# Row order of the loads of rotated queries and keys: 32 rows outermost, four parts within

## Chip, core and metric

One core of a Trainium2 chip runs one transformer layer. The metric is the time of one execution in microseconds of device time (us), the median of several. Before the change it is 2902.48 us, the median of three runs between 2901.76 and 2904.4.

## What is computed

A sequence of 1024 positions with 1024 features goes through a feed-forward block, a mixing block and a second feed-forward block. The mixing block holds two attentions: a differential one with 8 heads (phase "da" below) and one with 16 heads whose output is a gated sum of a compressed, a selected and a window branch (phase "ns"). The change touches only how queries and keys reach the score products. In the reference these are the lines

```python
s = jnp.einsum('bqhcd,bkhcd->bhcqk', qb, k).astype(jnp.float32) * scale      # da
s = jnp.einsum('bqgjd,bqgnld->bqgjnl', qb, kg).astype(jnp.float32) * scale   # ns, selected
s = jnp.einsum('bqgjd,bkgd->bqgjk', qb, kb).astype(jnp.float32) * scale      # ns, window
```

Each is a sum over the 64 features d of a head, after the rotation of queries and keys. The order of the terms in that sum is free.

## The kernel before

**Operands in two parts.** Products are taken to about single precision by cutting each operand into a rounded part and a remainder (`split`, L85 and L89: ScalarE, ACT in the profile, makes the rounded part, VectorE, DVE, the remainder). A weight product is three TensorE (PE) matmuls (L52 to L54).

**Rotated queries and keys pass through memory.** `rope_pair` computes two blocks of 128 columns of the input projection, rotates them, splits them and stores them (L635) to scratch tensors in device memory: `s_q` and `s_k` (one of each for every pair of da heads), `s_qns` for the ns queries, `s_kv` for the ns keys. Their shape is `[h, a, s, d, t]`:

- `h`: rounded part or remainder (queries have the rounded part once more at the end, so that `h = 0, 1` is rounded and remainder, and `h = 1, 2` remainder and rounded);
- `a`: first or second half of the 64 features, `s`: one of four vectors, `d`: 32 features, `t`: 1024 positions.

For a fixed `s`, the step from one `d` to the next is a row of 1024 numbers, 4 KB; the step from one `(h, a)` to the next is 4 x 32 x 1024 numbers, 512 KiB.

**Loads for the scores.** A score product contracts over 128 partitions: two `h` times two `a` times 32 `d`. The loads put them there in the order `(h a) d`, so that partition 32 j + d holds row d of part j. There are four places:

- `da_queries` (L928): four loads of 128 rows of 256 positions for each head and quarter of the sequence, a pool of 4 buffers (`B_DQ`), two loads to a buffer;
- `da_load_parts` (L1031): two key loads of 128 rows of 1024 positions for each head, a pool of 4 buffers (`B_DK`); the values `vt` follow at L1038;
- `ns_load_key` (L1047): four key loads of the same size, made during da head 4;
- `ns_queries` (L1072): two loads of 128 rows of 512 positions for each head and half.

`scores` multiplies (L909): the two passes of a score tile `S` use the queries with `h = 0, 1` and with `h = 1, 2` against the same key tile. Queries and keys of one product always come through the loads above, so their partitions are ordered alike. DVE then adds the mask and takes the row minimum (L916), ACT the exponential (L918); POOL and DVE scale, PE transposes (L964), ACT and DVE split again, and PE multiplies by the values (L991 to L993 in da, L1146 and L1147 in ns).

**Fillers.** Between score tiles the PE runs pieces of projections (`Filler`): units of `rope_pair` and `v_da_unit` for later heads, then gates. Their weights `wst` are loaded at L1200 and split by ACT at L1210 and DVE at L85. The value units end in transposes (L653), a split into `vh` and `vl`, and stores (L658); the gates in stores at L745. The finished da heads go out at L1018.

**What sets the order.** Every engine runs its instructions in the order of the program text as a scheduler laid it out at build time, and waits on semaphores. All transfers, loads and stores, are issued by SyncE (SP) alone, one after another; an issue that does not get through holds all later ones. A transfer is carried out by the core's 16 DMA engines.

Of the kernel before, what the change touches and what calls it, by code (L numbers as in the profile page):

```python
# [7 lines left out]
F32 = mybir.dt.float32  # L8
# [912 lines left out]
def da_queries(K, h, m):  # L921
    nc = K.nc
    qt = []
    p, s0 = h // 2, (h % 2) * 2
    for c in range(2):
        t = K.qp.tile([P, 2, 2 * P], F32R, tag="q", name="qt")
        for z in range(2):
            nc.sync.dma_start(out=t[:, z].bitcast(F32),  # L928
                              in_=K.s_q[p][z:z + 2, :, s0 + c, :, m * 256:(m + 1) * 256].rearrange("h a d t -> (h a) d t"))
        qt.append(t)  # L930
    return qt

# [88 lines left out]
def da_load(K, h):  # L1021
    drain([da_load_parts(K, h)])


def da_load_parts(K, h):
    nc = K.nc
    p, s0 = h // 2, (h % 2) * 2
    K.k = []
    for c in range(2):
        t = K.kp.tile([P, T], F32R, tag="k", name="kt")  # L1030
        nc.sync.dma_start(out=t.bitcast(F32), in_=K.s_k[p][:, :, s0 + c].rearrange("h a d t -> (h a) d t"))  # L1031
        K.k.append(t)
        yield
    K.v = []
    K.vv[h] = K.v
    for hl in range(2):
        t = K.vp.tile([P, 8, P], F32R, tag="v", name="vt")
        nc.sync.dma_start(out=t.bitcast(F32), in_=K.s_v[h][hl])  # L1038
        K.v.append(t)
        yield  # L1040


def ns_load_key(K, i):
    g, br = i // 2, i % 2
    pool, tag = [(K.rope, "cR"), (K.rope, "sR"), (K.mp, "m13"), (K.mp, "rh")][i]
    t = pool.tile([P, T], F32R, tag=tag, name="kt")
    order_after(K, K.nc.sync.dma_start(out=t.bitcast(F32), in_=K.s_kv[:, :, br * 2 + g].rearrange("h a d t -> (h a) d t")),  # L1047
                K.last)
    K.nk[g, br] = t

# [17 lines left out]
def ns_queries(K, hd, H):  # L1068
    qt = []
    for z in range(2):  # L1070
        t = K.qp[hd % 2].tile([P, TB], F32R, tag=f"q{z}", name="qt")
        K.nc.sync.dma_start(out=t.bitcast(F32), in_=K.s_qns[hd // 4][z:z + 2, :, hd % 4, :, H * TB:(H + 1) * TB]  # L1072
                            .rearrange("h a d t -> (h a) d t"))
        qt.append(t)
    return qt

# [89 lines left out]
def order_after(K, inst, first):  # L1166
    if first is not None:
        K.tc.add_manual_dep(inst.ins, first.ins.name,
                            mybir.DependencyInfo(mybir.DependencyClass.NoSync, mybir.DependencyReason.DATA),
                            reason="order the filler's weights")  # L1170
# [197 lines left out]
def da_phase(K, cg):  # L1368
    nc = K.nc
    with ExitStack() as ctx:  # L1370
        K.kp, K.vp, K.qp = open_pool(K, ctx, "dk", B_DK), open_pool(K, ctx, "dv", B_DV), open_pool(K, ctx, "dq", B_DQ)
        K.nk, K.vv = {}, {}
        for n, f in enumerate(da_units(K, 0)[:2] + da_units(K, 1)):
            if n == 2:
                early = da_load_parts(K, 0)
            if n >= 2:
                next(early)
            if n == 5:
                q0 = da_queries(K, 0, 0)
            drain([f()])  # L1380
# [29 lines left out]
        for p in range(4):  # L1410
            fill.pace(4 * (p + 1) if p < 2 else 8 + ng * (p - 1), PACE_DA)
            for h in (2 * p, 2 * p + 1):
                if h:
                    da_load(K, h)
                for m in range(4):
                    qt = q0 if h + m == 0 else da_queries(K, h, m)
                    if h == 4:
                        ns_load_key(K, m)
                    res = da_scores(K, h, m, qt, fill.step)
                    if pend:  # L1420
                        finish(*pend)
                    pend = (h, m, res)
            fill.end()
# [6 lines left out]
def ns_phase(K):  # L1430
    nc = K.nc
    K.low = LOW_NS
    with ExitStack() as ctx:
        K.qp, K.pcp = [open_pool(K, ctx, "nq0", 1)], [open_pool(K, ctx, "npc0", 1)]
        q0 = ns_queries(K, 0, 0)
        pc0 = ns_compressed(K, 0, 0)
        K.wslab = open_pool(K, ctx, "wsl", 1).tile([P, 5 * P], F32, name="wslab")
# [24 lines left out]
        for g in range(2):  # L1462
            for pr in range(4 * g, 4 * g + 4):
                for H in range(2):
                    pc = ns_compressed(K, pr, H) if pr + H else pc0
                    y = K.op.tile([P, TB], F32, tag="y", name="y")
                    for par in range(2):
                        hd = pr * 2 + par
                        qt = ns_queries(K, hd, H) if hd + H else q0
                        for m in (2 * H, 2 * H + 1):  # L1470
                            res = ns_scores(K, hd, m, qt, g, fill.step)
                            if pend:
                                finish(*pend)
                            pend = (hd, m, res, (pc, y), g, par)
# [242 lines left out]
```

## Time and profile before

| what | value |
|---|---|
| median of three runs | 2902.48 us |
| profiled execution: its time | 2903.55 us |
| profiled execution: first to last instruction (the span) | 2901.8 us |
| mean granted PE clock | 0.988 |
| TensorE busy (PE) | 2791.5 us, 96% |
| VectorE busy (DVE) | 1995.2 us, 69% |
| ScalarE busy (ACT) | 1370.8 us, 47% |
| GpSimd busy (POOL) | 789.2 us, 27% |
| DMA: moved, mean share of the 16 engines | 476.12 MB, 48.1% for the kernel's own queue |

Names like `kt<-sk` mean "writes tile kt, reads sk". In a timeline row stand the start, the time taken, engine, line, operation and tiles, and in brackets how long the engine stood idle before it and what ended that. "SPq" is SyncE issuing a transfer: the time in its row is that of the issue, not of the transfer. In a row of stages stand the stretch, then each engine's busy time with its count of instructions, the granted PE clock, the mean busy share of the 16 DMA engines, and GB/s. The da phase runs from about 930 to 1480 us, the ns phase to about 2060 us; the feed-forward blocks lie before and behind.

### The profile page before, as it was taken

What the parts mean: (1) busy time and instruction counts of PE and PEld (TensorE: products, weight loads), DVE (VectorE), ACT (ScalarE), POOL (GpSimd) and SP (SyncE); (2) the same over time, 40 slices, a digit from 0 to 9 for tenths busy, and PEclk for the clock granted to TensorE, in tenths of its full rate; (3) what the DMA queues carried; (4) which work ended last, traced back from release to release, by engine and by line L of the source; (5) the groups of instructions that cost most, each with busy time, mean ns of one, the idle gap of its engine ahead of it and who ended that gap; (6) DMA issues with size and microseconds to landing.
All of it is one profiled execution on the core that took longest, in us unless ns stands there. A gap on an engine that the chain in (4) does not pass through costs nothing. (4 is left out here: it accounts for less than half of the span.)

```text
span 2901.8 us, 40199 instructions
## 1 busy us (share of the span) xinstructions
PE 2791.5 (96%) x14278; PEld 2055.0 (71%) x14278; DVE 1995.2 (69%) x3356; ACT 1370.8 (47%) x2351; POOL 789.2 (27%) x701
## 2 busy tenths in 40 slices
PE   8999999999999899989989999999999999999998
PEld 6644447887788778868877778888787844444886
DVE  7866865666688467667777777777333977676566
ACT  7533424442333245445566666677433653333443
POOL 3134321000045212322233333333242414223001
PEclk9999999999999999999999999999999999999999
DMA  4355547655446645444432226222843246445854
GB/s 164 121 202 179 177 170 269 217 189 148 153 174 211 221 155 177 167 162 160 155 122 89 88 80 201 88 88 81 315 149 120 80 146 221 163 171 172 293 182 144
DMA packets 212137, 476.12 MB, mean 164 GB/s; under 512 B 20832, under 2 KB 39520, under 8 KB 211936
## 3 DMA queue, kind: packets, MB, share of 16 engines
q1 hardware_dynamic: 211936, 473.55, 48.1%
q8 instruction: 112, 1.84, 0.3%
q14 instruction: 89, 0.73, 0.1%
HBM read 312.52 MB, written 160.96 MB: 163 GB/s over the span
## 5 line engine op out<-in xcount | busy, mean ns | idle before, releaser
L405 PEld LDWEIGHTS <-w 128*128 128x128 f16 x3024 | 297.3, 99 | 381.8 <-issue 32.2
L52 PE MATMUL gm<-hi,whi 128*128 128x512 f32 x880 | 351.0, 399 | 6.0 <-ACT whi L89 3.3
L54 PE MATMUL gm<-hi,wlo 128*128 128x512 f32 x880 | 348.7, 397 | 0.5 <-DVE wlo L85 0.5
L53 PE MATMUL gm<-lo,whi 128*128 128x512 f32 x880 | 348.0, 395 | 0.0
L405 PE MATMUL Y<-tf,w 128*128 128x512 f16 x1296 | 297.5, 384 | 16.7 <-DVE u L443 13.9
L909 PE MATMUL S<-kt,qt 128*128 128x320 f32 (+5 forms) x1152 | 270.1, 352 | 27.2 <-ACT Pt L918 12.4
L85 DVE TENSOR_TENSOR wlo<-st,whi 128x1024 fp32r<-128x1024 f32 x154 | 197.6, 1301 | 114.2 <-ACT whi L89 113.2
L916 DVE CUSTOM_DVE_ANT_0 S<-S,slab 128x896 f32<-128x896 f32 (+7 forms) x320 | 224.3, 710 | 56.1 <-PE S L909 50.3
L53 PE MATMUL acc<-wlo,whi 128*128 128x512 f32 (+1 forms) x628 | 244.4, 389 | 1.0 <-DVE wlo L85 1.0
L89 ACT ACTIVATE whi<-st 128x1024 fp32r<-128x1024 f32 x154 | 160.7, 1057 | 178.8 <-PE acc L54 106.4
L54 PE MATMUL acc<-whi,wlo 128*128 128x512 f32 (+1 forms) x628 | 243.0, 390 | 0.0
L52 PE MATMUL acc<-whi 128*128 128x512 f32 (+1 forms) x628 | 240.7, 387 | 0.4 <-DVE xd L590 0.4
L970 DVE TENSOR_TENSOR tl<-tr,th 128x512 f16<-128x512 f32 (+2 forms) x304 | 183.9, 616 | 45.9 <-ACT th L969 44.9
L909 PEld LDWEIGHTS S<-kt,qt 128*128 128x128 f32 x1152 | 182.7, 190 | 43.9 <-ACT Pt L918 14.6
L1098 POOL TENSOR_SCALAR Ps<-Ps,l 128x384 f32<-128x384 f32 (+7 forms) x128 | 102.0, 797 | 372.6 <-DVE l L1096 246.0
L969 ACT ACTIVATE th<-tr 128x512 f16<-128x512 f32 (+2 forms) x304 | 159.2, 539 | 79.0 <-PE tr L964 62.6
L405 PE MATMUL X<-h,w 128*128 128x512 f16 x864 | 195.3, 379 | 0.6 <-ACT s L415 0.5
L52 PEld LDWEIGHTS gm<-hi,whi 128*128 128x128 f32 x880 | 168.1, 191 | 39.0 <-ACT whi L89 3.5
L54 PEld LDWEIGHTS gm<-hi,wlo 128*128 128x128 f32 x880 | 167.8, 191 | 36.3 <-DVE wlo L85 1.4
L53 PEld LDWEIGHTS gm<-lo,whi 128*128 128x128 f32 x880 | 167.7, 191 | 30.8
L85 DVE TENSOR_TENSOR wlo<-wst,whi 128x1024 fp32r<-128x1024 f32 x103 | 137.9, 1340 | 45.6 <-ACT whi L89 36.8
L521 POOL TENSOR_TENSOR u<-u,u 128x512 f32<-128x512 f32 x36 | 52.8, 1467 | 345.0 <-DVE sa L102 163.2
(330 smaller groups left out, 6167.9 us busy)
## 6 DMA issues: line engine op xcount, KB each, us to landing
wst<-in_win_dram SPq DMA_DIRECT2D x55, 512.0 KB
sw<-w2s SPq DMA_DIRECT2D x44, 512.0 KB
st<-sw SPq DMA_DIRECT2D x88, 256.0 KB
st<-saT SPq DMA_DIRECT2D x88, 256.0 KB
a<-in_f1w_dram SPq DMA_DIRECT2D x36, 512.0 KB
a<-in_f2w_dram SPq DMA_DIRECT2D x36, 512.0 KB
st<-saB SPq DMA_DIRECT2D x66, 256.0 KB
qt<-sq SPq DMA_DIRECT2D x128, 128.0 KB
```

What stands on the lines that cost most here:

```text
L52: first = nc.tensor.matmul(out, lhsT=w[0][:, wk], rhs=x[0], start=start, stop=False, skip_group_check=skip)
L53: nc.tensor.matmul(out, lhsT=w[0][:, wk], rhs=x[1], start=False, stop=False, skip_group_check=skip)
L54: nc.tensor.matmul(out, lhsT=w[1][:, wk], rhs=x[0], start=False, stop=stop, skip_group_check=skip)
L85: return nc.vector.tensor_tensor(out=lo, in0=src, in1=hi.bitcast(F32), op=ALU.subtract)
L89: nc.scalar.activation(out=hi, in_=src, func=AF.Copy)
L405: K.mark = nc.tensor.matmul(o, lhsT=w[:, a, m * h + k], rhs=x[k][:, b], start=start and k == 0 and i == 0, stop=k == h - 1 and i == 2, ski ...
L521: nc.gpsimd.tensor_tensor(out=a, in0=a, in1=b, op=ALU.mult)
L909: K.last = nc.tensor.matmul(S[:, o:o + n], lhsT=q, rhs=k[:, k0 + c:k0 + c + n], start=i == 0, stop=i == 1)
L916: nc.vector.tensor_tensor_reduce(out=sv, in0=sv, in1=mv, scale=-0.125, scalar=BIG, op0=ALU.add, op1=ALU.min, accum_out=nm)
L969: nc.scalar.activation(out=hi[:, 0:n], in_=tr[:, 0:n], func=AF.Copy)
L970: nc.vector.tensor_tensor(out=lo[:, 0:n], in0=tr[:, 0:n], in1=hi[:, 0:n], op=ALU.subtract)
L1098: nc.gpsimd.tensor_scalar(out=p[:, 0:n], in0=p[:, 0:n], scalar1=l[:, c:c + 1], scalar2=P_NS, op0=ALU.mult, op1=ALU.mult)
```

## The change

All four loads take their 128 rows as `d (h a)` in place of `(h a) d`: partition 4 d + j now holds row d of part j. Queries and keys change alike, so each product of the contraction still meets its partner, in another order. Bytes, row lengths, counts of transfers and tiles stay as they were, and the instructions of every engine, SP's transfers among them, stand in the same order as before. In the access pattern that a load carries for its source, the outermost count goes from 4 (parts, 512 KiB apart) to 32 (rows, 4 KB apart), with the other one within; the destination is 128 partitions in both.

```diff
@@ da_queries
-  in_=K.s_q[p][z:z + 2, :, s0 + c, :, m * 256:(m + 1) * 256].rearrange("h a d t -> (h a) d t"))
+  in_=K.s_q[p][z:z + 2, :, s0 + c, :, m * 256:(m + 1) * 256].rearrange("h a d t -> d (h a) t"))
@@ da_load_parts
-  nc.sync.dma_start(out=t.bitcast(F32), in_=K.s_k[p][:, :, s0 + c].rearrange("h a d t -> (h a) d t"))
+  nc.sync.dma_start(out=t.bitcast(F32), in_=K.s_k[p][:, :, s0 + c].rearrange("h a d t -> d (h a) t"))
@@ ns_load_key
-  order_after(K, K.nc.sync.dma_start(out=t.bitcast(F32), in_=K.s_kv[:, :, br * 2 + g].rearrange("h a d t -> (h a) d t")),
+  order_after(K, K.nc.sync.dma_start(out=t.bitcast(F32), in_=K.s_kv[:, :, br * 2 + g].rearrange("h a d t -> d (h a) t")),
@@ ns_queries
   K.nc.sync.dma_start(out=t.bitcast(F32), in_=K.s_qns[hd // 4][z:z + 2, :, hd % 4, :, H * TB:(H + 1) * TB]
-                      .rearrange("h a d t -> (h a) d t"))
+                      .rearrange("h a d t -> d (h a) t"))
```

## Prediction

> **What bounds the kernel now.** I read the page first, then the stages.
>
> ```profile
> PE 2791.5 (96%) x14278; PEld 2055.0 (71%) x14278; DVE 1995.2 (69%) x3356; ACT 1370.8 (47%) x2351; POOL 789.2 (27%) x701
> 930.00:1420.00 490.00, 454.48 (x2303) 380.99 (x2302) 328.23 (x653) 216.12 (x431) 133.21 (x127) 0.97 0.50 174
> 1490.00:2050.00 560.00, 549.02 (x3729) 450.94 (x3728) 427.67 (x1109) 376.83 (x863) 181.21 (x248) 1.00 0.33 107
> ```
>
> PE bounds the kernel. A faster load can only give back time in which PE stands still or runs at a lowered clock. The second and third rows are the stages in which the changed loads run: da, then ns. In da PE is busy for 454.48 of 490 us, 35.5 us idle, at a granted clock of 0.97. In ns it is idle for 11.0 of 560 us at full clock. So what can be won lies in da.
>
> The next view is how the DMA engines carry these loads; the last two numbers of each stage row are the mean busy share of the 16 engines and GB/s.
>
> ```profile
> 968.00:976.00 8.00, 7.71 (x35) 5.97 (x33) 4.64 (x6) 3.07 (x3) 0.80 (x2) 1.00 0.25 88
> 977.00:978.00 1.00, 0.00 (x0) 0.00 (x0) 0.00 (x0) 0.00 (x0) 1.00 (x2) 1.00 1.04 408
> 966.37 4.57 SPq L1031 DMA_DIRECT2D kt<-sk  x4
> 970.98 7.74 SPq L635 DMA_DIRECT2D sq<-rh  x2
> kt<-sk SPq DMA_DIRECT2D x16, 512.0 KB
> kt<-skv SPq DMA_DIRECT2D x4, 512.0 KB
> qt<-sq SPq DMA_DIRECT2D x128, 128.0 KB
> qt<-sqn SPq DMA_DIRECT2D x64, 256.0 KB
> ```
>
> From 968 to 976 us only key loads are under way, four of them issued from 966.37 on, and the share is 0.25: four of 16 engines, as many as the load's pattern has outermost parts. When a store with 128 outermost rows joins them (977 to 978) all 16 are busy. The Trainium skill ("DMA: Bandwidth & Descriptors", section "Why a DMA increments its semaphore by 16 and not by 1") says that a transfer uses the largest number of engines up to 16 that divides the outermost counts of both its patterns. By that, 4 and 128 give 4, as seen, and the new 32 and 128 give 16; no row of before has a pattern with 32.
>
> By the rows alone the new count lies between the 4 of four outermost parts and the 16 of 128 outermost rows. I take 16, since 32 is more than there are engines, as 128 is.
>
> At 88 GB/s over four engines, 22 GB/s each, a key load of 512 KB takes 5.96 us, a da query load of 128 KB 1.49 us, an ns query load of 256 KB 2.98 us. In da that is 128 x 1.49 + 20 x 5.96 = 310 us on the same four engines. The stage moves 174 GB/s x 490 us = 85.3 MB in all; the changed loads are 27.3 MB of it, and a sixteenth of the other 58.0 MB is 3.6 MB, 165 us at 22 GB/s. So the four engines work 475 of 490 us, the twelve others 165. The mean of that, 0.495, is the 0.50 of the row. In ns it is 191 us for the changed loads and 122 us for a sixteenth of the rest, 313 of 560: busy, but not full.
>
> Full engines hold SP, which issues every transfer in order:
>
> ```profile
> L928 SPq DMA_DIRECT2D qt<-sq x128: 509/532/8288, 927.9 to 1429.8; - x128
> L1072 SPq DMA_DIRECT2D qt<-sqn x64: 509/526/537, 1444.5 to 1989.6; - x64
> L635 SPq DMA_DIRECT2D sqn<-rh x16: 360/424/1355, 807.3 to 907.7; - x16
> L635 SPq DMA_DIRECT2D sq<-rh x16: 360/464/5365, 920.1 to 1199.5; - x16
> ```
>
> An issue takes about half a microsecond, in da up to 8.3 us; the ns loads never exceed 0.54. The same store line (third and fourth row) took at most 1.36 us before da and up to 5.37 in it. A 512 KB store or weight load behind a key load then lands late though its own engines 4 to 15 are free, since it is finished only when its part on the four full ones is.
>
> **The change part by part.** It adds no instruction and moves none; it takes each changed load from four engines to 16. Where PE waits for that, I followed each PE stop of da that a transfer ends, directly or through ACT:
>
> ```profile
> 980.13 0.69 PE L909 MATMUL S<-kt,qt 128*128 128x128 f32 x2 [4.08 <-DMA kt<-sk]
> 1291.16 0.55 PE L991 MATMUL o<-th,vt 128*128 128x256 f32 x1 [2.73 <-DMA vt<-sv]
> 1390.53 0.70 PE L909 MATMUL S<-kt,qt 128*128 128x320 f32 x3 [0.94 <-DMA qt<-sq]
> 1023.85 0.33 PE L653 MATMUL tr<-ident,vt 128*128 128x128 f32 x1 [2.14 <-DVE vt L650]
> 1019.77 0.60 ACT L89 ACTIVATE vh<-tr 128x512 fp32r<-128x512 f32 x1 [4.33 <-DMA sk<-rh]
> 1195.25 0.58 PE L991 MATMUL o<-th,vt 128*128 128x256 f32 x1 [3.33 <-ACT th L89]
> 1193.66 1.06 ACT L1210 ACTIVATE whi<-wst 128x1024 fp32r<-128x1024 f32 x1 [6.05 <-DMA wst<-in_win_dram]
> 1185.33 5.04 SPq L1031 DMA_DIRECT2D kt<-sk  x1
> 1190.47 1.15 SPq L1200 DMA_DIRECT2D wst<-in_win_dram  x1
> 1272.72 1.22 PE L909 MATMUL S<-kt,qt 128*128 128x512 f32 x2 [6.09 <-ACT Pt L918]
> 1271.51 0.60 ACT L89 ACTIVATE vh<-tr 128x512 fp32r<-128x512 f32 x1 [6.04 <-DMA sv<-vh]
> 1253.11 5.37 SPq L1031 DMA_DIRECT2D kt<-sk  x1
> 1258.57 0.42 SPq L658 DMA_DIRECT2D sv<-vh  x1
> ```
>
> Direct stops, 4.08 + 2.73 + 0.94 = 7.75 us. The first waits for the second of two key loads: two at 5.96 us from about 967.5 on end at 979.4. On 16 engines at the same rate they take 2 x 1.49 = 2.98 us and end near 970.5, before PE gets there at 976.05 (980.13 less 4.08); even eight engines would do, with 2 x 2.98 us to 973.5. The other two wait for values and queries queued on the same four engines.
>
> Stops through ACT, 2.14 + 3.33 + 6.09 = 11.56 us. At 1023 a value split sits behind a store of keys that had not landed. At 1195 the split scores `th` stand on ACT behind the weight split, which waits for weights that SP could issue only after 5.04 us on a key load. At 1272 the exponential stands behind `vh`, whose buffer is freed by a store issued at 1258.57, behind a key load that took 5.37 us to issue. All three lose their cause.
>
> Clock: each long stop is followed by a stretch at half the granted clock. The second number is PE's busy time in it.
>
> ```profile
> 978.70:985.50 6.80, 5.37 (x14) 4.30 (x15) 2.02 (x6) 0.46 (x2) 0.37 (x1) 0.50 0.81 265
> 1193.80:1200.60 6.80, 5.35 (x13) 4.30 (x14) 5.24 (x10) 4.16 (x9) 1.89 (x3) 0.50 0.39 143
> 1268.80:1275.60 6.80, 2.88 (x11) 2.69 (x12) 2.94 (x8) 2.32 (x6) 0.00 (x0) 0.50 0.32 120
> 1289.30:1296.10 6.80, 4.94 (x12) 4.02 (x13) 5.75 (x10) 2.76 (x6) 3.70 (x4) 0.50 0.65 210
> ```
>
> Work at half clock takes twice as long, so half of 5.37 + 5.35 + 2.88 + 4.94 = 18.54 us, 9.3 us, comes back if the stops go.
>
> All together: 7.75 + 11.56 + 9.3 = 28.6 us at most from these six stops. What is late next: behind the direct stops nothing is known to be, and with their two clock stretches (5.37 and 4.94, half of it 5.2) they give 12.9 us. Behind the three others stands ACT and DVE work that has to be done in any case: the `th` of 1195 and the exponential of 1272 cost some 0.60 to 1.06 us, as `vh` and `whi` in the rows above, once their turn comes, and their inputs come from PE itself. I take three quarters of their 11.56 + 4.1 = 15.7 us, 11.8. Sum: 24.7, rounded to 24.5 us. Bounds: 12.9 us if only the direct ones go; above 28.6 I allow for 36, all of the 35.5 us that PE is idle in the stage, since SP, no longer held, issues everything behind earlier.
>
> Nothing is paid in ns: PE's 11 us of idle time there are not ended by these loads, and the four engines at 313 of 560 us do not hold SP. SP's issue of a changed load (median 0.53 us against 0.42 or 0.46 of a store) may get shorter or stay; SP is not what PE waits for once it isn't held, so this costs or gives nothing.
>
> The profiled execution took 2903.55 us for a span of 2901.8, and lies 1.07 above the median of 2902.48. From the former the sum gives 2879.05, for the median 2878.0. A difference of 0.2%, 5.8 us, is about what a measurement of this kernel can tell from none.
>
> **The rivals.**
>
> *The stops pass to the next in line.* ACT and DVE may turn out to have been almost as late as the transfers at 1023, 1195 and 1272, so that only the direct stops go. For it speaks that in da ACT and DVE each stand in one fixed row of unlike work; against it that they are busy for 216 and 328 of 490 us. Gain 12.9 us or somewhat less, as a stop of 1 to 2 us may keep a half-clock stretch: about 2891.
>
> *The loads stay on four engines.* If the count of engines is not taken from the outermost count of the source, nothing changes: 2902.5. Against it: four parts and a share of 0.25 fit exactly.
>
> *The rows get slow.* A load's neighbouring rows now lie 512 KiB apart in memory, and 16 engines walk them in step. If such rows take more than four times as long each, a key load is longer than 5.96 us again, but on all 16 engines, so that weights and stores wait wherever they run. At eight times the four-engine stalls double: PE's 19.3 us of stops and 9.3 us of clock come once more, 28.6 us, and the time is 2931. Decisive is whether a key load takes over 5.96 us. Against it: each engine's rows keep their lengths and lay 4 KB apart already, and stores that fill scratch with two rows 512 KiB apart for each partition (`sq<-rh`) reach the full share at 977. The Trainium skill ("DMA: Bandwidth & Descriptors", section "Latency and other measured facts") states that rows at a pitch of 512 KiB still moved 207 GB/s against 214 at best, and that the rate halves only at 4 MiB. By that a load would lose 3% and this rival fall away; no row of before shows a load with such a pattern.
>
> **How the numbers follow.** The forecast, with most of the six stops gone, gets 0.74; stops passed on 0.13; four engines still 0.08; slow rows 0.05. The first two are faster by more than 5.8 us, so faster is 0.87, same 0.08, slower 0.05. The forecast's own range is 36 us of gain to 16.8 (the direct 12.9 and a quarter of 15.7), 2866 to 2886; with most of the passed-on case it goes to 2894, and what is left out is the last two rivals and the ends.
>
> **What would show it.** Right: a share near 1 and over 300 GB/s while key loads alone run, no issue in da above about 2 us, the kernel's DMA share unchanged over the stage at 0.5; PE starting its second score product near 976 without a wait for keys; the half-clock stretches near 980, 1195, 1270 and 1290 gone, the mean clock above 0.988; the ns stage as long as now. Wrong: key loads at a share of 0.25, or PE's idle time in da near 35 us again with ACT or DVE named in place of the transfers, or packets that move fewer GB/s at the full share.

## The result, and the profile after

The changed kernel takes 2862.23 us (median of four runs, 2860.35 to 2862.45) against 2902.81 us for the kernel before, measured beside it (2901.76 to 2904.4). The ratio is 0.9858, with a 95% interval of 0.9841 to 0.9875: 40.6 us less. The direction was forecast, the size was not: the forecast was 24.5 us of gain, and 2862.23 lies below the range's lower end of 2866. The profiled execution took 2862.03 us, its span is 2860.2 us, and its mean granted clock 0.994.

The page of the changed kernel: span, busy times, and the line on DMA packets.

```profile
span 2860.2 us, 40199 instructions
PE 2775.8 (97%) x14278; PEld 2046.7 (72%) x14278; DVE 1998.2 (70%) x3356; ACT 1371.7 (48%) x2351; POOL 791.9 (28%) x701
DMA packets 214681, 476.13 MB, mean 166 GB/s; under 512 B 23376, under 2 KB 42064, under 8 KB 214480
```

The work is the same: as many instructions on every engine, as many bytes. PE's busy time is 15.7 us shorter than before (2791.5) although its 14278 matmuls are the same ones: less of the work was done at a lowered clock.

The stages of the changed kernel: da, ns, and four microseconds in which key loads are the main traffic. Behind the busy times stand the granted clock, the DMA engines' share and GB/s.

```profile
930.00:1420.00 490.00, 479.79 (x2520) 406.03 (x2518) 360.31 (x713) 238.12 (x475) 146.49 (x138) 1.00 0.55 185
1490.00:2050.00 560.00, 546.76 (x3668) 448.69 (x3667) 411.63 (x1045) 365.10 (x822) 178.55 (x236) 1.00 0.36 126
962.00:966.00 4.00, 4.00 (x20) 3.30 (x19) 1.15 (x2) 0.73 (x1) 2.54 (x2) 1.00 1.01 390
```

In 490 us of da PE is idle for 10.2 us instead of 35.5, and the clock is 1.00 instead of 0.97. That is 25.3 us of idle time; the clock is worth the 9.3 us that the prediction works out from its four half-clock stretches (0.03 x 490 = 14.7 us would count time in which PE stood still a second time). Together it is 34.6 us more of work at full clock in the same 490 us. The key loads now run at a share of 1.01 and 390 GB/s, where the row of before had 0.25 and 88.

The first rows of what PE waits for between 930 and 1490, in us in total, times, longest:

```profile
PE S L909 <- ACT Ps L918: 7.4, 1, 7.4
PE S L909 <- ACT Pt L918: 4.6, 7, 1.2
PE tot L1008 <- ACT sq L1001: 2.0, 2, 1.2
PE o L992 <- DVE tl L85: 1.1, 3, 0.6
PE tr L653 <- DVE vt L650: 1.0, 1, 1.0
```

No transfer is named any more. The longest, 7.4 us, is the switch from da to ns; it is there before the change as well. The issues of changed loads on SP (shortest, median and longest in ns), and PE where it used to stand 4.08 us for the second key load:

```profile
L928 SPq DMA_DIRECT2D qt<-sq x128: 512/556/1554, 925.3 to 1388.2; - x128
L1072 SPq DMA_DIRECT2D qt<-sqn x64: 513/520/1236, 1402.8 to 1948.5; - x64
L1031 SPq DMA_DIRECT2D kt<-sk x16: 513/598/836, 959.5 to 1326.2; - x16
```

```profile
971.41 0.22 PE L909 MATMUL S<-kt,qt 128*128 128x128 f32 x1
...
971.98 0.44 PE L909 MATMUL S<-kt,qt 128*128 128x128 f32 x3
```

No bracket stands behind the rows: PE did not wait. The longest issue of a query load fell from 8.29 to 1.55 us.

**Where the 41.5 us between the two profiled executions are.** Both kernels run the same 14278 matmuls in the same order, so each can be compared with itself. The table gives by how much the lead of the changed kernel grows across each stretch, with times of before.

| stretch of before, us | what stood there | lead grows by, us |
|---|---|---|
| 0 to 925 | nothing that the change touches | 2.7 |
| 925 to 965 | | 0.6 |
| 965 to 987 | stop for the second key load, and its clock | 7.34 |
| 987 to 1012 | stop of 2.68 at 1014.25, in part (the table goes by starts) | 2.10 |
| 1016 to 1028 | stop at 1023.85 | 2.67 |
| 1075 to 1090 | stops at 1081.36 and 1085.89 | 2.96 |
| 1130 to 1140 | stop at 1135.57 | 1.63 |
| 1185 to 1202 | stop at 1195.25, and its clock | 5.56 |
| 1265 to 1280 | stop at 1272.72, and its clock | 7.52 |
| 1280 to 1286.5 | stop at 1287.46 | 1.45 |
| 1286.5 to 1297 | stop for the values, and its clock | 5.29 |
| 1380 to 1395 | stop for queries | 1.80 |
| 1490 to 2880 | ns and all behind it | 0.3 |

What stands between these stretches adds up to a loss of 0.4 us. All of the change's gain lies in da. The first 2.7 us come before any changed load: they are the difference between two executions (ahead of 925 us the clock stands at half for 17.1 us in the trace of before and for 6.8 us in that of after), and other kernels below, with the same work up to there, are between 1.8 us behind and 3.9 us ahead of the one of before at that point.

### The profile page after: what moved, and what is told of

The parts are those of the page before. It is cut to its first block, busy times and chain, and to the rows that moved or that the text cites. A ratio compares the mean times of both kernels' runs of the same rounds, so it can differ in the third digit from the quotient of the medians.

```text
span 2860.2 us, 40199 instructions
## 1 busy us (share of the span) xinstructions
PE 2775.8 (97%) x14278; PEld 2046.7 (72%) x14278; DVE 1998.2 (70%) x3356; ACT 1371.7 (48%) x2351; POOL 791.9 (28%) x701
## 2 busy tenths in 40 slices
DMA packets 214681, 476.13 MB, mean 166 GB/s; under 512 B 23376, under 2 KB 42064, under 8 KB 214480
```

## The experiments

The theory at the start: changed loads went through four DMA engines, and whatever had to pass these four came late; on 16 engines nothing does. Rivals: it is the order of the rows in the tile or in memory that matters; it is SP, held on its issues, and not the engines; and, for the size, it is the key loads alone or the query loads alone.

**One phase at a time.** The new order for L928 and L1031 alone (da), then for L1047 and L1072 alone (ns):

```diff
 # da alone: L928 and L1031 as after the change, these two as before
+.rearrange("h a d t -> (h a) d t")   # L1047, L1072
-.rearrange("h a d t -> d (h a) t")
```

> Only the da queries and da keys take the new row order; ns queries and ns keys keep the old one. Theory A (a load runs on as many DMA engines as its outermost count allows, and four full engines make every other transfer late and hold SyncE): nearly the whole gain, 2862 to 2872 us, since of the ns loads only the four key loads (four times about 6 us on four engines) fall into the da stage. Theory B (only the landing of the changed loads themselves counts): the same time. Rival that the ns stage gives part of the gain: 2880 or more.

> Only the ns queries and ns keys take the new row order. Theory A: 2892 to 2903 us; the ns stage stays as it is, and at most the stops near 1270 and 1290 us, when the ns keys are loaded, get shorter. Theory B: 2902. Rival that the ns stage gives part of the gain: 2890 or less with a shorter ns stage.

Measured: da alone 2864.67 us, ratio 0.9876 (0.9861 to 0.9891); ns alone 2892.49 us, ratio 0.997 (0.9959 to 0.998). The da loads carry the gain. What the ns loads give alone is not given in ns: compared matmul by matmul, it comes between 1265 and 1297, where the four ns key loads run beside da, and the ns stage keeps its length. With both the ns loads add nothing that shows, since that same place is cured by the da loads.

**Queries alone, keys alone.** The new order at L928 only, and at L1031 only. The partitions of queries and keys then no longer match, so these two kernels compute other da scores, with the same instructions and bytes.

```diff
 # queries alone, against the kernel before
-.rearrange("h a d t -> (h a) d t")   # L928; for keys alone: L1031
+.rearrange("h a d t -> d (h a) t")
```

> Only the da queries take the new row order, so queries and keys of da no longer match by partition and the da scores are not the reference's. Theory A: the four engines lose three quarters of 191 us and work about 332 of the da stage's 490 us; key loads still come two to four in a row at 6 us each, so the stop at 980 us and some behind key loads stay: 2872 to 2888 us. Theory B: only the one stop for queries (0.9 us) goes: 2898 to 2903.

> Only the da keys take the new row order (da scores again not the reference's). Theory A: the four engines lose three quarters of 95 us and work about 403 of 490 us; the rows of key loads that held SyncE up to 5.4 us are gone, the stop at 980 us with them: 2870 to 2886 us. Theory B: the stop at 980 us with its clock stretch goes, 6.8 us: 2894 to 2897.

Measured: queries alone 2881.88 us, ratio 0.9936 (0.9921 to 0.995); keys alone 2873.4 us, ratio 0.9909 (0.9893 to 0.9926). Neither does it alone, and their 19 and 27 us make more than the 36 of both (da alone): some stops go by either change. If only the landing of the changed loads themselves counted, 2898 to 2903 and 2894 to 2897 us were expected; that falls. One thing came out other than expected: with queries alone the stop for the second key load, which was to stay, shrinks from 4.08 to 1.40 us, so part of it seems to have been query loads on the same engines. With queries alone, key loads are still on four engines, and PE still stops at the place that was 1195 before. The rows are of that kernel: PE's stop, ACT's wait in front of it, and SP's issues ahead of that.

```profile
1187.70 0.58 PE L991 MATMUL o<-th,vt 128*128 128x256 f32 x1 [3.79 <-ACT th L89]
```

```profile
1186.10 1.06 ACT L1210 ACTIVATE whi<-wst 128x1024 fp32r<-128x1024 f32 x1 [6.51 <-DMA wst<-in_win_dram]
```

```profile
1170.42 0.55 SPq L1031 DMA_DIRECT2D kt<-sk  x1
...
1173.06 1.03 SPq L1200 DMA_DIRECT2D wst<-in_win_dram  x1
...
1177.09 0.81 SPq L1031 DMA_DIRECT2D kt<-sk  x1
1181.20 0.35 SPq L1200 DMA_DIRECT2D wst<-in_win_dram  x1
```

SP is not held here: no issue in these rows takes over 1.03 us, and yet the weights have landed only 13 us after their issue. ACT's wait is on the semaphore of the load issued at 1173.06. A transfer over all 16 engines raises its semaphore 16 times, once for each engine's part, and the trace has the time of each. Here they are for this weight load, and for the store that `vh` waits for (at 1272 in the kernel before):

```
weight load          issued     parts 1 to 12 landed    parts 13 to 16 landed
before               1181.07    1186.68 to 1187.45      1192.88 to 1193.57
queries alone        1173.06    1179.03 to 1179.39      1184.42 to 1186.02
after                1161.47    all 16: 1167.58 to 1168.94

store of vh          issued     parts 1 to 12 landed    parts 13 to 16 landed
before               1258.57    1260.47 to 1260.62      1270.81 to 1271.43
queries alone        1246.30    1248.13 to 1248.37      1259.66 to 1260.97
after                1228.91    all 16: 1230.82 to 1231.76
```

Twelve parts are there, and four come 5 to 13 us later. ACT goes on 0.1 us after the sixteenth (1193.66 and 1271.51 in the kernel before). The trace does not name the engine of a part; that the four late ones are those of the four engines that still have key loads to do is read from their number, and from their being late no more once the loads run on 16.

With keys alone the rest of the pattern shows. Its PE rows, at the place of 1291 before:

```profile
1258.45 0.97 PE L909 MATMUL S<-kt,qt 128*128 128x384 f32 x4 [2.31 <-ACT Pt L918]
1262.20 0.55 PE L991 MATMUL o<-th,vt 128*128 128x256 f32 x1 [2.78 <-DMA vt<-sv]
```

The values still come late: 2.78 us against 2.73 before. Query loads and ns key loads are still on the four engines here. Either must go for this stop to go: compared matmul by matmul, queries alone wins 5.29 us there (as the whole change does) and ns alone 4.96.

**Old order, 16 engines.** The tile keeps its old order, and each load is cut into four transfers of one part of 32 rows, 32 outermost.

```diff
+def load_rows(nc, t, src):
+    return [nc.sync.dma_start(out=t[(h * 2 + a) * 32:(h * 2 + a + 1) * 32].bitcast(F32), in_=src[h, a])
+            for h in range(2) for a in range(2)]
```

> The old row order in the tiles, but each of the four kinds of load is cut into four transfers, one for each part, with 32 rows outermost. Theory A (the number of engines): 16 engines, so about the time of the changed kernel in spite of three times 212 more issues (some 160 us more of SyncE's time in the da stage): 2860 to 2880 us. Theory C (it is the order of rows in memory or in the partitions that counts): 2900 to 2905, as before.

Measured: 2862.53 us, ratio 0.9869 (0.9853 to 0.9886): the same as the change. The order of rows, in memory and in the tile, is worth nothing by itself that shows; the engines are. (Compared matmul by matmul, 35.9 of the 38.5 us of da are won here; 1.5 of the rest is a stop of 1.3 us for values, which stays.) SP has 636 more issues here (three more for each of 212 loads) and has time for them:

```profile
930.00:1420.00 490.00, 478.45 (x2510) 404.61 (x2508) 358.65 (x711) 236.95 (x472) 145.04 (x137) 1.00 0.59 185
```

**Old order, two engines.** Each load is two transfers of two parts, 2 outermost: if the count of engines is what costs, two must cost far more than four.

```diff
+def load_rows(nc, t, src):
+    return [nc.sync.dma_start(out=t[h * 64:(h + 1) * 64].bitcast(F32), in_=src[h]) for h in range(2)]
```

> The old row order, each load cut into two transfers of two parts with two outermost. Theory A: both run on the same two engines; in the da stage these would have 2 x 310 + 165 = 785 us of work for a stage of 490, so the stage gets longer by some 250 to 330 us: 3130 to 3250 us, a DMA share of 0.12 while key loads run alone; the ns stage (2 x 191 + 122 = 504 of 560 us) grows little. Theory B (own landing only): the direct stops double or treble, 2910 to 2940. Theory C: 2900 to 2905.

Measured: 3141.53 us, ratio 1.0827 (1.0811 to 1.0843), 239 us slower. The stages: key loads alone, then da. Then what PE waits for there.

```profile
975.00:993.00 18.00, 9.04 (x40) 7.14 (x39) 5.47 (x8) 3.07 (x3) 5.02 (x4) 0.85 0.12 48
930.00:1420.00 490.00, 356.56 (x1641) 293.27 (x1640) 231.25 (x444) 145.14 (x285) 99.43 (x91) 0.85 0.37 130
```

```profile
PE S L909 <- ACT Pt L918: 34.8, 10, 12.4
PE o L994 <- ACT th L89: 27.7, 2, 16.2
PE S L909 <- DMA qt<-sq: 23.3, 6, 7.4
PE S L909 <- DMA kt<-sk: 17.6, 2, 14.1
PE o L994 <- DMA vt<-sv: 14.8, 3, 7.3
```

The share is 0.12, two engines of 16, at 48 GB/s. The waits are of the kinds that the kernel before has, each several times as long (its longest for keys 14.1 us against 4.1, for values 7.3 against 2.7): the stops grow with the work that each of the loaded engines has.

With 2, 4, 8 (below) and 16 engines at a share of 0.12, 0.25, 0.48 and 1.01, the runs agree with the rule of the Trainium skill that the prediction names ("DMA: Bandwidth & Descriptors", section "Why a DMA increments its semaphore by 16 and not by 1"), that the engines are as many as the largest number up to 16 that divides both outermost counts. The traces also count them transfer by transfer, whatever else is under way: after the change all 1429 transfers raise their semaphores 16 times each, 22864 in all. Before it is 2332 less, 11 for each of the 212 changed loads, which leaves 5. With loads over eight engines it is 7 less for each (5936 for 848), which leaves 9, and with two 13 less (5512 for 424), which leaves 3: always one more than the engines.

**SP held, engines free.** The change, and behind each head's key load twelve transfers of one number out of the key tile, which SP cannot issue before the keys have landed, and which then take it some time.

```diff
+        for i in range(12 * c):
+            nc.sync.dma_start(out=K.s_held[h][i:i + 1], in_=t[0:1, i:i + 1].bitcast(F32))
```

> The changed kernel, with twelve transfers of one number each behind each head's key load, which read that key tile and so wait for it and then take about a third of a microsecond each to issue: SyncE is held some 5 us per head, 45 us in all, while the DMA engines stay free. If holding SyncE was what cost the time (about 95 us of holding went with the change): a third to a half of the stops through ACT and DVE come back, 2870 to 2882 us. If it was transfers that land late on full engines, though issued: 2861 to 2866.

Measured: 2861.75 us, ratio 0.9865 (0.9848 to 0.9881): nothing lost. The hold turned out smaller than meant. All its issues, and a long run of them:

```profile
L1033 SPq DMA_DIRECT2D shd<-kt x96: 214/251/833, 965.5 to 1340.2; - x96
```

```profile
973.65 3.57 SPq L1033 DMA_DIRECT2D shd<-kt  x8
```

96 x 0.25 us is 24 us of SP's time, in pieces such as the 3.57 us of this row, where the kernel before has single issues of up to 8.29. So the run shows that SP can lose this much for nothing, not that it could lose all. For the rest, queries alone is the better witness. SP's issue rows between 930 and 1420 add up to 245.8 us before, 154.6 after, 166.4 with queries alone: there SP is nearly as free as after the change (single issues of up to 4.5 us are left), and half of the gain is still missing.

**New order, cut by rows.** The tile as after the change, but each load cut into four transfers of 8 rows times four parts, 8 outermost.

```diff
+def load_rows(nc, t, src):
+    return [nc.sync.dma_start(out=t[i * 32:(i + 1) * 32].bitcast(F32),
+                              in_=src[:, :, i * 8:(i + 1) * 8].rearrange("h a d t -> d (h a) t"))
+            for i in range(4)]
```

> Each changed load is cut into four transfers of 8 rows (times four parts), 8 outermost: eight engines, in the new row order. Theory A with a threshold (stops come only when engines are full): the eight engines work 310/2 + 165 = 320 of the da stage's 490 us, so nearly the time of the changed kernel, 2860 to 2872 us. If instead the loss grows in step with the load of the fullest engines (242, 320, 475 us for 16, 8 and 4): a third of the gain is lost, about 2876. The cut reorders some hundred other instructions, so 5 us either way tell nothing.

Measured: 2925.74 us, ratio 1.0084 (1.0065 to 1.0102). The expectation missed: slower than before the change, by the same count of transfers that cost nothing when the cut went by parts. The rows are of this kernel: key loads alone, da, PE's first waits from 930 to 1490, the issues of da query loads, and a stretch of SP.

```profile
966.50:976.50 10.00, 9.02 (x43) 7.34 (x42) 6.16 (x11) 3.99 (x7) 2.79 (x3) 1.00 0.48 166
930.00:1420.00 490.00, 455.30 (x2299) 380.01 (x2297) 331.04 (x644) 214.72 (x427) 137.14 (x129) 0.97 0.50 171
```

```profile
PE S L909 <- DMA qt<-sq: 15.4, 14, 2.3
PE tr L969 <- DVE Pt L957: 5.5, 7, 1.6
```

```profile
L922 SPq DMA_DIRECT2D qt<-sq x512: 646/646/1342, 927.0 to 1463.0; - x171
```

```profile
1320.86 11.03 SPq L922 DMA_DIRECT2D qt<-sq  x16
1331.99 0.38 SPq L745 DMA_DIRECT2D smx<-vt  x1
```

The share while key loads run is 0.48: eight engines, and half the speed. But what PE waits for are query loads, and SP issues them without a pause, 16 in 11.03 us. An issue of this shape takes 0.646 us; one of a single part of 32 rows takes 0.419:

```profile
L922 SPq DMA_DIRECT2D qt<-sq x512: 302/419/1918, 920.0 to 1395.2; - x171
```

(this row is of the old order on 16 engines). Two causes were left, eight engines and SP's time, and two more kernels take them apart: only the key loads cut, and only the query loads cut.

> The new order, but each key load (16 in da, 4 for ns) is cut into four transfers of 8 rows times four parts, 8 outermost; query loads are single transfers as after the change. It separates two theories of why the same cut of all loads took 2925.74 us. Theory 1, SP's issue time: a transfer of this shape takes SP 0.646 us to issue, so a query load costs 2.6 us of SP instead of 0.52; key loads are few (60 more issues, 60 x 0.65 = 39 us of SP over the whole stage, on top of the 154.6 of 490 that SP is busy after the change), so SP never becomes late and the time is 2860 to 2872, with no PE stop named by a query load. Theory 2, eight engines: a key load on half of the engines lands late (share 0.48 while key loads run), and that made the loss: 2895 to 2925 here. Theory 3, in between: stops like those at four engines but half as long, 2872 to 2890.

> The new order, but each query load (128 in da, 64 in ns) is cut into four transfers of 8 rows times four parts, 8 outermost; key loads are single transfers as after the change. SP has 384 more issues in da and all 512 take 0.646 us, 331 us against 67. Theory 1, SP's issue time: 2915 to 2930 as with all loads cut, SP busy for 400 us or more of 930 to 1420, PE's stops named by query loads. Theory 2, key loads on eight engines made the loss: 2860 to 2880. The engines' orders differ a little from those after the change here (as with all loads cut), and a part of a loss may be due to that; if it is only that, PE's stops are named by DVE, ACT or POOL and not by query loads.

Measured: only keys 2863.5 us, ratio 0.9864 (0.9846 to 0.9883); only queries 2892.54 us, ratio 0.9974 (0.9962 to 0.9985). Key loads on eight engines cost nothing: the lead over the kernel before grows stretch by stretch as after the change, 38.8 us from 925 to 1490 against 38.5. The second theory falls. Cutting the queries costs 30 us against the change, well short of the 2915 to 2930 us expected, and with query loads among the waits again. That query loads run on eight engines here cannot be the reason: on four, in keys alone, they cost 9 us against da alone (2873.4 and 2864.67). The da stage of only queries, its hundred microseconds from 1100 and from 1300, PE's first wait on a transfer and the issues:

```profile
930.00:1420.00 490.00, 467.61 (x2417) 392.47 (x2416) 344.90 (x680) 226.40 (x455) 140.90 (x134) 0.99 0.52 176
...
1100.00:1200.00 100.00, 97.77 (x530) 82.73 (x528) 77.17 (x159) 52.25 (x108) 30.45 (x30) 1.00 0.52 174
...
1300.00:1400.00 100.00, 89.94 (x465) 74.95 (x464) 69.81 (x147) 51.98 (x111) 24.93 (x27) 0.95 0.44 144
```

```profile
PE S L909 <- DMA qt<-sq: 5.2, 7, 1.3
```

```profile
L922 SPq DMA_DIRECT2D qt<-sq x512: 654/655/1282, 924.6 to 1432.0; - x171
```

The sum of SP's issue rows in each hundred microseconds tells the kernels apart:

| kernel | 1000 to 1100 | 1100 to 1200 | 1200 to 1300 | 1300 to 1400 | time, us |
|---|---|---|---|---|---|
| after | 28.6 | 36.2 | 34.1 | 32.4 | 2862.23 |
| only keys cut by rows | 34.0 | 45.0 | 53.1 | 35.8 | 2863.5 |
| all loads cut by parts | 64.3 | 72.7 | 75.9 | 75.7 | 2862.53 |
| only queries cut by rows | 85.9 | 90.5 | 88.4 | 89.8 | 2892.54 |
| all loads cut by rows | 90.4 | 88.3 | 90.2 | 87.7 | 2925.74 |

Up to 76 of 100 us SP's issues are free; at about 90, by this reading, SP is the bound, and what it falls behind adds up until the stage ends: PE loses little before 1200 and 10 of 100 us after 1300. Why cutting the keys costs nothing by itself and 33 us on top of cut queries follows from the same table, since there SP has no time left for 60 more issues; but this was argued, not tried. These last two kernels also differ in the order of some hundred instructions of the other engines, and what part of the loss that has stays open.

## Why the prediction was wrong in size

- **The bound and, in the main, the mechanism were right.** PE bounds, four engines carried the loads, 16 do now, nothing is paid in ns, no row got slow. Of what was to show it, the share (1.01 at 390 GB/s while keys load), the second score product without a wait (971.98), the four half-clock stretches and the length of ns came as written; the longest issue of a changed load is 1.55 us, of any transfer in da 1.77. The stage's share was to stay at 0.5 and rose to 0.55, as more of the work falls into the same 490 us. The rows of the half-clock places in the changed kernel:

```profile
970.00:977.00 7.00, 7.00 (x34) 5.81 (x34) 4.69 (x10) 2.86 (x6) 3.90 (x3) 1.00 0.64 188
1168.00:1175.00 7.00, 6.76 (x39) 5.71 (x38) 6.39 (x10) 2.55 (x6) 6.82 (x6) 1.00 0.61 221
1235.00:1242.00 7.00, 6.79 (x50) 6.14 (x49) 5.75 (x15) 3.66 (x9) 2.85 (x5) 1.00 0.40 147
1249.00:1256.00 7.00, 7.00 (x40) 5.81 (x39) 5.87 (x14) 6.27 (x13) 0.70 (x1) 1.00 0.74 222
```

- **The direct stops** were put at 12.9 us with their clock; 7.34 + 5.29 + 1.80 = 14.4 came. A small miss.
- **The step that failed first: "I take three quarters" of the stops through ACT.** All of it came, 2.67 + 5.56 + 7.52 = 15.75 us of 15.7. (That it is so near is in part luck: the stop at 1195 gave 0.5 us less than was put down for it and its clock, the one at 1023 0.5 more.) ACT and DVE were not next in line: with the transfer early, PE does not wait at these places at all. The quarter, 3.9 us, was taken off without a row that shows a second late input.
- **The step that failed second: the list of stops.** It took "each PE stop of da that a transfer ends, directly or through ACT", and did not follow the others back from the engine that PE's row names. Five more, that name DVE or ACT, went too (the one at 1014.25 in part, 1.01 of its 2.68 us stay), 2.10 + 2.96 + 1.63 + 1.45 = 8.1 us. The one at 1135.57 (1.63) goes with two engines too, where all else gets worse, so the count of engines does not explain it. The one at 1287.46 (1.45) goes with queries alone and with ns alone; its chain was not traced. The one at 1014.25 (2.10) goes with keys alone and not with queries alone. The rows of the kernel before have its chain, ACT, DVE and PE:

```profile
994.93 1.06 ACT L89 ACTIVATE rh<-m 128x1024 fp32r<-128x1024 f32 x1 [13.22 <-DMA sq<-rh]
```

```profile
996.16 1.23 DVE L85 TENSOR_TENSOR rl<-m,rh 128x1024 fp32r<-128x1024 f32 x1 [12.65 <-DMA sq<-rl]
...
1013.51 0.69 DVE L650 TENSOR_TENSOR vt<-gm,R 128x512 f32<-128x512 f32 x1
```

```profile
1014.25 0.66 PE L653 MATMUL tr<-ident,vt 128*128 128x128 f32 x4 [2.68 <-DVE vt L650]
```

  ACT and DVE stand for two stores that SP issued behind the four key loads of 966.37. What this leaves undone keeps DVE at work from 1003.19 until `vt`, with one pause of 0.76 us, and PE waits for `vt`. With queries alone the two waits are still 13.06 and 11.95 us; with keys alone they are gone.

  For the pair at 1081 and 1085 the chain is of the same kind. The kernel before, ACT, DVE and PE, in order of time:

```profile
1077.72 1.06 ACT L1210 ACTIVATE whi<-wst 128x1024 fp32r<-128x1024 f32 x1 [8.13 <-DMA wst<-in_win_dram]
```

```profile
1078.82 1.23 DVE L85 TENSOR_TENSOR wlo<-wst,whi 128x1024 fp32r<-128x1024 f32 x1 [4.89 <-ACT whi L1210]
1080.62 0.68 DVE L85 TENSOR_TENSOR tl<-tr,th 128x512 fp32r<-128x512 f32 x1
```

```profile
1081.36 0.39 PE L992 MATMUL o<-tl,vt 128*128 128x256 f32 x1 [1.12 <-DVE tl L85]
```

  PE's row names `tl`, a piece of DVE work with no transfer in it. But DVE had stood 4.89 us for `whi`, and ACT 8.13 us for weights. DVE has no pause from there to 1085 either. Read at PE's row alone this is compute, and the prediction's list does not have it.
- **The upper bound left out the clock.** "All of the 35.5 us that PE is idle" was the most that was allowed for. A stop costs its idle time and the half-clock stretch behind it, and the prediction itself had 9.3 us of that; 35.5 + 9.3 = 44.8 would have put the lower end at 2857.7 and held the result.
- **A cause was misread where the size was right.** At 1195 and 1272 the prediction has weights and a store that SP issued late, behind key loads of 5.04 and 5.37 us. The weights that ACT waited for had been issued at 1181.07, ahead of that key load; and the store of 1258.57 had twelve of its parts done 2 us later. Both waited for four parts on the full engines. The prediction describes this way of being late ("finished only when its part on the four full ones is") and then did not use it. Queries alone shows the difference: SP free, the stop still there.
- **The sum.** 24.5 forecast, 3.9 for the quarter, 1.5 for the direct stops, 8.1 for the five others, 0.6 between 925 and 965, and 2.7 of difference between two executions ahead of da: 41.3, of 41.5 between the profiled executions.
- **The rivals.** Stops passed to the next in line: none. Loads that stay on four engines: no, by the share. Slow rows: no. On the rows' 512 KiB pitch the Trainium skill ("DMA: Bandwidth & Descriptors", section "Latency and other measured facts") has 207 GB/s against 214 at best, so next to no loss. The runs agree: the changed order and the old order cut by parts take the same time, and key loads move 390 GB/s.

## What to carry to other kernels

Read the outermost count of each transfer's pattern, and the share while it runs alone: a load on few engines costs most through others, since every transfer that spreads over all engines waits for its part on the full ones. For the size, follow a PE stop back until a transfer or PE itself ends the wait, not one link, and count the clock behind a stop into the bound as well as into the sum. Cutting a load into more transfers to spread it is free only while the queue that issues has time: here up to 76 of 100 us, and, by the reading above, no longer at 90.

## What was not expected of the hardware

- The time that SP takes to issue a load depends on the load's pattern more than on its bytes: 0.42 us for one part of 32 rows, 0.52 to 0.60 for the 128 rows of a whole load, and 0.65 for 8 rows of four parts, which has the 32 partitions and the bytes of the first.
- Each engine that takes part adds one small packet of its own to a transfer: packets under 512 B went from 20832 to 23376, by 2544, which is 212 changed loads times 12 more engines. It cost nothing that shows.
- Eight engines did as well as 16 for the key loads (2863.5 and 2862.23 us); four cost 17 us (queries alone, 2881.88, against da alone, 2864.67). How fast one load is decided less here than how long the others have to wait for its engines: of the 38.5 us of da, 9.1 are at the stops for key and query loads themselves (7.34 and 1.80).
